# Gate exponents of four mLSTM heads: from selector and mask matmuls to transfers and a GpSimd fill

## The chip, the core and the metric

The kernel runs on one core of one Trainium2 chip. A core has TensorE (PE: matmuls, with the weight load PEld beside it), VectorE (DVE), ScalarE (ACT), GpSimd (POOL) and SyncE (SP), each with its own instruction queue, worked off in order. SP and POOL issue transfers here. The metric is device time in microseconds (us), the median of the runs; lower is better.

## The reference

A trunk of two layers over 512 tokens of width 1024: layer A (four mLSTM heads beside four memory-attention heads, then a gated MLP), layer B (band attention beside memory attention, then a gated MLP), all in float32. The change sits in the mLSTM heads. Per chunk and head the reference computes

```
b = cumsum(lf)                                 # lf: log forget gate, ii: log input gate
d = b[t] - b[s] + ii[s]   where s <= t, else -inf
m_t = max(b + m_st, max_s d)
s = (q k^T) * exp(d - m_t)
num = s v + inter * (q C);   den = sum(s) + inter * (q n)
h = num / max(|den|, exp(-m_t))
```

so each head needs a 512 by 512 lower-triangular matrix of exp(row term + column term): one term depends on the key token s, the other on the query token t, and entries with s > t are zero.

## The kernel before

Every float32 product is made of three float32r matmuls over a high and a low part (`mm3`, lines 176 to 180): high by high (L178), high by low (L179), low by high (L180). The parts come from `split` (lines 133 to 135): ScalarE copies the high part (L134) and VectorE subtracts for the low part (L135). Weights of 512 KB each arrive in three `wr` buffers by SP's queue and are split into three `wh` and three `wl` buffers. PSUM has three `pmm`, three `psc` and two `ptr` banks.

Keys lie on the 128 partitions, in four blocks s = 0 to 3; block s has the queries from s*128 on, so 512, 384, 256 and 128 columns. `gate_rows` (line 1005) makes the gate terms: scans on VectorE on 4 partitions (one per head), then for each block s the row term of each query in `rr`, at 4 partitions of a 128-partition tile (L1053, L1062, VectorE). Lines 1067 to 1071 split these rows into a high and a low part in `rp`, two float32r tiles with zeros elsewhere (memsets L1029 on GpSimd). The column term, on the key partitions, is `acol` (L1075 to L1077, by PE transposes).

In `mlstm_head`, `weighted_scores(s)` puts head h's row term on all 128 partitions with a matmul of a 0/1 selector `sels` against `rp` (L1134, into a `psc` bank), adds a mask of 0 and -1e30 for the block on the diagonal with a second matmul, identity against mask (L1135), and ScalarE takes exp with `acol` as bias out of that bank (L1137). Then PE makes the scores into another `psc` bank (`mm3` and two L517), VectorE multiplies them with the exp (L1143), and the result is split into `pt`. `products(s)` multiplies `pt` with the values into two `ptr` banks. The selectors, the identity and the mask in float32r are made once at the start (lines 101 to 118).

The order on the engines is made by a scheduler from the program's order, except where `pin` keeps it or `manual_schedule` sets it. Each head is a generator whose steps are woven with projections of other tiles (`weave`, lines 1202 to 1223): PE has projection matmuls to do between a head's steps. `gate_rows` is woven with the value projections and the tiles of heads 0 and 1 and finished before head 0 starts. `head_queries` (line 494) needs two GpSimd memsets (L497) for each of its four calls in layer A.

The pool tag `bias` has two buffers of 128 x 512, used only from layer B on (L1301, L1383).

Of the kernel before, what the change touches and what calls it, by code (L numbers as in the profile page):

```python
# [16 lines left out]
P = 128  # L17
D = 1024
S = 512
# [27 lines left out]
def f(ap):  # L47
    return ap.bitcast(F32)
# [3 lines left out]
def trunk(  # L52
# [22 lines left out]
    pool = ctx.enter_context(tc.tile_pool(name="pool", bufs=1))  # L75
    psum = ctx.enter_context(tc.tile_pool(name="psum", bufs=1, space=bass.MemoryType.PSUM))

    bufs = {"wr": 3, "wh": 3, "wl": 3, "u": 57, "t": 8, "pt": 2, "s": 16, "rb": 3, "bias": 2}
    pbufs = {"mm": 3, "sc": 3, "tr": 2}
    count = [0]  # L80
    dram = ctx.enter_context(tc.tile_pool(name="dram", bufs=1, space=bass.MemoryType.DRAM))
# [1 line left out]
    def sb(tag, shape, dtype=F32):  # L83
        count[0] += 1
        return pool.tile(shape, dtype, tag=tag, name=f"{tag}{count[0]}", bufs=bufs[tag])
# [12 lines left out]
    V.memset(ones, 1.0)  # L98
    onesr = cpool.tile([P, P], F32R, name="onesr")
    V.tensor_copy(onesr, ones)  # L100
    identr = cpool.tile([P, P], F32R, name="identr")
    V.tensor_copy(identr, ident)
    maskf = cpool.tile([P, P], F32, name="maskf")
    G.memset(maskf, 0.0)

# [1 line left out]
        out=maskf, in_=maskf, pattern=[[1, P]], base=0, channel_multiplier=-1,  # L107
        compare_op=ALU.is_ge, fill=NEG,
    )
    maskr = cpool.tile([P, P], F32R, name="maskr")  # L110
    V.tensor_copy(maskr, maskf)

    sels = [cpool.tile([P, AH, P], F32R, name=f"sel{i}") for i in range(2)]
    for i, sel in enumerate(sels):
        G.memset(f(sel), 0.0)
        for s in (2 * i, 2 * i + 1):
            q = slice(32 * s, 32 * s + AH)
            V.tensor_copy(sel[q], ident[q, 32 * s : 32 * s + AH].unsqueeze(2).to_broadcast([AH, AH, P]))

    mcf = cpool.tile([P, 3, 2], F32, name="mcf")  # L120
    V.memset(mcf, 0.0)
    V.memset(mcf[:, 0, 0:1], 1.0)
# [78 lines left out]
    def chain(*gens):  # L201
        for g in gens:
            yield from g
# [796 lines left out]
    floor2 = cpool.tile([P, TT, AH], F32, name="floor2")  # L1000
    RO = [0, 512, 896, 1152, 1280]

    rp = []

    def gate_rows():

# [17 lines left out]
        yield  # L1024
        lfr, br, ar, mr = (sb("t", [P, S])[:AH, :] for _ in range(4))
        rr = [sb("t", [P, S]) for _ in range(2)]
        rp.extend(sb("u", [P, S], F32R) for _ in range(2))
        for t in rp:
            G.memset(f(t), 0.0)  # L1029
        pin(V.tensor_copy(lfr, lfp[:AH, :]))  # L1030
        yield
        for T in range(TT):
# [14 lines left out]
        for s in range(TT):  # L1047
            off = None
            for T in range(s, TT):
                sl = slice(T * P, (T + 1) * P)  # L1050
                dst = rr[s // 2][64 * (s % 2) : 64 * (s % 2) + AH, sl]
                if T == s:
                    pin(V.tensor_scalar(dst, mr[:, sl], -1.0, None, op0=ALU.mult))  # L1053
                else:
                    end = br[:, T * P - 1 : T * P]
                    if off is None:
                        off = end
                    else:
                        k = 4 + 4 * s + T - s
                        V.tensor_tensor(out=tot[:, k : k + 1], in0=off, in1=end, op=ALU.add)  # L1060
                        off = tot[:, k : k + 1]
                    V.tensor_scalar(dst, mr[:, sl], -1.0, off, op0=ALU.mult, op1=ALU.add)  # L1062
            yield
        pin(V.tensor_tensor(out=mr, in0=mr, in1=br, op=ALU.add))
        V.tensor_scalar(mr, mr, -40.0, None, op0=ALU.max)
        yield
        for s in range(TT):
            q, t = 64 * (s % 2), rp[s // 2]
            src, hi = rr[s // 2][q : q + AH, s * P :], t[q : q + AH, s * P :]
            pin(V.tensor_copy(hi, src))  # L1070
            V.tensor_tensor(out=t[q + 32 : q + 32 + AH, s * P :], in0=src, in1=f(hi), op=ALU.subtract)
            yield
        tp = ps("tr")
        for T in range(TT):
            nc.tensor.transpose(tp[:, T * AH : (T + 1) * AH], ar[:, T * P : (T + 1) * P], ident[:AH, :AH])  # L1075
# [44 lines left out]
    def a_memory_queries(hp):  # L1120
        memq[hp] = queries((yield from project(w_in, 4 * AW + 2 * AH + hp * P, act)), None)

    def mlstm_head(h):
        hp, odd = divmod(h, 2)
        sh = 3 * hp + 1
# [4 lines left out]
        def weighted_scores(s):  # L1130
            n = S - s * P
            sl = slice(s * P, (s + 1) * P)
            r = ps("sc")
            nc.tensor.matmul(r[:, :n], sels[s % 2][:, h, :], rp[s // 2][:, s * P :], start=True, stop=False)  # L1134
            nc.tensor.matmul(r[:, :P], identr, maskr, start=False, stop=True)  # L1135
            e = sb("t", [P, S])
            A.activation(e[:, :n], r[:, :n], AF.Exp, bias=acol[:, s, h : h + 1])  # L1137
            yield
            o = ps("sc")
            kf, qf = ks[full], qs[full]  # L1140
            mm3(o[:, :n], kf[0][:, sl], kf[1][:, sl], qf[0][:, s * P :], qf[1][:, s * P :], True, False)
            head_scores(o[:, :n], odd, qs[sh], slice(s * P, S), ks[sh], sl, False, True)
            V.scalar_tensor_tensor(e[:, :n], o[:, :n], DH**-0.5, e[:, :n], op0=ALU.mult, op1=ALU.mult)  # L1143
            split(pt[:, RO[s] : RO[s + 1]], pt[:, 1280 + RO[s] : 1280 + RO[s + 1]], e[:, :n])
            yield
# [15 lines left out]
        yield from weighted_scores(2)  # L1161
        yield from products(0)
        yield from weighted_scores(3)
        yield from products(1)
        yield from products(2)
        yield from products(3)
        sqs = []
        for o, j, r in ((nums[0], full, slice(0, P)), (nums[1], sh, rs)):
# [2 lines left out]
            sqs.append(sq)  # L1171
            V.tensor_tensor(out=og[j][r, :], in0=o[r, :], in1=og[j][r, :], op=ALU.mult)
        yield
        st = ps("sc")
        for T in range(TT):
            sl = slice(T * P, (T + 1) * P)
# [25 lines left out]
    fill = gate_rows()  # L1202
    weave(chain(value_columns(0), a_tiles(0, 1)), fill, 0.3)
    run(fill)
    fill = chain(a_tiles(2), a_memory_queries(0), a_tiles(3, 4), a_tiles(5), a_memory_queries(1))
    memkv = load_memory_kv(0)
    weave(mlstm_head(0), fill, 1.4)
# [293 lines left out]
```

## Time and profile before

| what | value |
|---|---|
| median of 3 runs | 1211.98 us (1211.79 to 1214.2) |
| span of the profiled execution, first to last instruction | 1209.9 us |
| TensorE busy | 1196.0 us, 99% of the span, 7063 matmuls |
| VectorE, ScalarE, GpSimd busy | 945.1, 711.1, 125.3 us |
| granted TensorE clock, mean | 0.999 |
| L1134, first and last start | 106.3 (weight load) to 240.2 us, 16 times |

The profile is of one execution. Its own time is given only as the span, 1209.9 us, which lies 2.1 us below the median of the runs; what lies around the span is not itemised. Busy time of TensorE counts a matmul from its start to the end of its pipeline, which overlaps the next one; how fast matmuls follow one another is read from the differences of their starts. A row of the timeline is: start (us), duration (us), engine, line, operation, tiles written and read, shapes, count, and, in brackets, the idle time before it and who ended it.

### The profile page before, as it was taken

How to read it: one execution, taken by the hardware profiler on the slowest of the kernel's cores; microseconds unless marked ns; L12 is line 12 of the kernel's file. 1: busy time of each engine (PE TensorE's matmuls, PEld its weight loads, DVE VectorE, ACT ScalarE, POOL GpSimd, SP SyncE). 2: the span in 40 equal slices, each digit the busy share in tenths (PEclk: the TensorE clock that was granted, in tenths of full speed). 3: DMA queues.
4: the chain of work that ended last, by engine and by line, in shares of the span. 5: the costliest groups of instructions: out<-in, count | busy, mean ns of one | idle time of the engine just before them, and what ended most of it. 6: DMA issues, size and time to landing. Idle time of an engine off the chain costs nothing.

```text
span 1209.9 us, 18791 instructions
## 1 busy us (share of the span) xinstructions
PE 1196.0 (99%) x7063; PEld 1058.6 (87%) x7063; DVE 945.1 (78%) x1733; ACT 711.1 (59%) x1251; POOL 125.3 (10%) x197
## 2 busy tenths in 40 slices
PE   9999999999999999999999999999999999999997
PEld 9988888888889999999988888878889999999986
DVE  7878688877978777777698888997896777777755
ACT  4536577644655555555475667775565555555545
POOL 1300000001011111111011000001101001111100
PEclk9999999999999999999999999999999999999999
DMA  8634111347556676665563323145845466666551
GB/s 276 207 98 122 54 53 57 109 138 187 129 137 160 145 160 150 161 141 133 143 195 109 99 72 94 57 129 167 199 97 139 107 138 139 140 140 134 120 156 70
DMA packets 205260, 159.14 MB, mean 132 GB/s; under 512 B 7960, under 2 KB 185586, under 8 KB 205170
## 3 DMA queue, kind: packets, MB, share of 16 engines
q1 hardware_dynamic: 184338, 120.78, 34.1%
q0 software_dynamic: 20832, 37.17, 16.5%
q8 instruction: 55, 0.90, 0.3%
q14 instruction: 35, 0.29, 0.1%
HBM read 129.42 MB, written 32.44 MB: 134 GB/s over the span
## 4 chain that ended last, share of the span: by engine, by line
PE 94%; ACT 3%; DVE 2%; issue 0%; ACTq 0%; DVEq 0%
PE pmm L178 18%; PE pmm L180 18%; PE pmm L179 18%; PE ptr L178 6%; PE ptr L179 6%; PE ptr L180 6%; PE psc L180 5%; PE psc L178 5%; PE psc L179 5%; PE psc L517 2%; PE ptr L1328 1%; ACT wh L134 1%; PE ptr L1349 1%; PE ptr L1350 1%; PE ptr L586 0%; PE ptr L600 0%
## 5 line engine op out<-in xcount | busy, mean ns | idle before, releaser
L178 PE MATMUL pmm<-u,wh 128*128 128x512 f32 (+1 forms) x968 | 337.1, 349 | 0.1
L180 PE MATMUL pmm<-u,wl 128*128 128x512 f32 (+1 forms) x968 | 333.6, 345 | 0.0
L179 PE MATMUL pmm<-u,wh 128*128 128x512 f32 (+1 forms) x968 | 333.3, 345 | 0.1
L135 DVE TENSOR_TENSOR wl<-wr,wh 128x1024 fp32r<-128x1024 f32 (+4 forms) x168 | 194.7, 1160 | 96.7 <-ACT wh L134 96.0
L134 ACT CAST wh<-wr 128x1024 fp32r<-128x1024 f32 (+4 forms) x168 | 168.0, 1002 | 99.9 <-PE pmm L179 47.2
L180 PEld LDWEIGHTS pmm<-u,wl 128*128 128x128 f32 x968 | 183.6, 190 | 21.1
L179 PEld LDWEIGHTS pmm<-u,wh 128*128 128x128 f32 x968 | 183.9, 190 | 18.0 <-DVE u L135 0.8
L178 PEld LDWEIGHTS pmm<-u,wh 128*128 128x128 f32 x968 | 183.7, 190 | 17.7 <-ACT u L134 0.5
L178 PE MATMUL ptr<-u,wh 128*128 128x512 f32 x272 | 106.7, 392 | 0.0
L179 PE MATMUL ptr<-u,wh 128*128 128x512 f32 x272 | 106.5, 392 | 0.0
L180 PE MATMUL ptr<-u,wl 128*128 128x512 f32 x272 | 105.8, 389 | 0.0
L748 POOL DMA_DIRECT2D xspill<-t x64 | 56.0, 875 | 411.4 <-ACT t L747 408.6
L178 PE MATMUL pmm<-u,u 128*128 128x256 f32 x296 | 84.5, 285 | 2.5 <-ACT t L824 2.5
L180 PE MATMUL pmm<-u,u 128*128 128x256 f32 x296 | 84.0, 284 | 0.4 <-DVE u L135 0.4
L179 PE MATMUL pmm<-u,u 128*128 128x256 f32 x296 | 83.8, 283 | 0.0
L135 DVE TENSOR_TENSOR u<-pt,u 128x512 fp32r<-128x512 f32 x102 | 69.9, 688 | 9.7 <-ACT u L134 7.1
L178 PE MATMUL psc<-u,wh 128*128 128x256 f32 (+1 forms) x232 | 76.1, 328 | 0.0
L179 PE MATMUL psc<-u,wh 128*128 128x256 f32 (+1 forms) x232 | 75.9, 327 | 0.0
L747 ACT COPY t<-ptr 128x512 f32<-128x512 f32 x64 | 37.5, 586 | 65.3 <-PE ptr L180 65.3
L135 DVE TENSOR_TENSOR u<-t,u 128x512 fp32r<-128x512 f32 x78 | 53.4, 689 | 21.4 <-ACT u L134 21.1
L134 ACT CAST u<-pt 128x512 fp32r<-128x512 f32 x102 | 63.2, 619 | 11.4 <-DVE pt L859 11.1
L921 ACT ACTIVATE t<-t 128x512 f32<-128x512 f32 x34 | 21.6, 635 | 80.2 <-DVE t L657 80.2
(290 smaller groups left out, 2568.0 us busy)
## 6 DMA issues: line engine op xcount, KB each, us to landing
wr<-in_ffn_w_up_dram SPq DMA_DIRECT2D x54, 512.0 KB, 5.0
wr<-in_ffn_w_down_dram SPq DMA_DIRECT2D x38, 512.0 KB, 3.8
pt<-in_ffn_w_up_dram SPq DMA_DIRECT2D x34, 512.0 KB, 6.8
xspill<-t POOLq DMA_DIRECT2D x64, 256.0 KB, 4.8
wr<-in_a_w_in_dram SPq DMA_DIRECT2D x20, 512.0 KB, 3.8
xspill<-u POOLq DMA_DIRECT2D x32, 256.0 KB, 3.0
u<-xspill SPq DMA_DIRECT2D x32, 256.0 KB, 4.9
wr<-in_w_kv_dram SPq DMA_DIRECT2D x12, 512.0 KB, 4.1
```

The lines of the kernel that those rows point to most:

```text
L134: high = A.copy(hi, src) if on_act else V.tensor_copy(hi, src)
L135: low = V.tensor_tensor(out=lo, in0=src, in1=f(hi), op=ALU.subtract)
L178: nc.tensor.matmul(o, lh, rh, start=first, stop=False, skip_group_check=more)
L179: nc.tensor.matmul(o, lh, rl, start=False, stop=False, skip_group_check=more)
L180: nc.tensor.matmul(o, ll, rh, start=False, stop=last, skip_group_check=more)
L517: nc.tensor.matmul(o, a, b, start=first and i == 0, stop=i == 1)
L747: A.copy(t, o)
L748: G.dma_start(xspill[j], t, accum_op=ALU.add)
L921: A.activation(self.acc, self.acc, AF.Silu)
L1328: nc.tensor.transpose(tp[:, b * P : (b + 1) * P], es[T, h][:, b * P : (b + 1) * P], ident)
L1349: nc.tensor.matmul(o2[:, s * P :], w, hi_at(pts[h], s, s, TT - s), start=s == 0, stop=False)
L1350: nc.tensor.matmul(o2[:, s * P :], w, lo_at(pts[h], s, s, TT - s), start=False, stop=s == TT - 1)
```

## The change

`gate_rows` no longer splits the rows into `rp`, and the memsets of `rp`, the selectors and the float32r identity and mask are gone. When a block's rows stand in `rr`, GpSimd's queue writes its four rows to a DRAM tile `rowd` (4 transfers). `exponents(h, s)` reads one row back with a step of zero over the partitions, so that all 128 partitions of a `bias` buffer hold it; `masked(h, s)` is a GpSimd affine_select that fills the 128 x 128 block on the diagonal with -1e30 where the query lies before the key. ScalarE's exp reads that buffer instead of a `psc` bank. Head 0's four loads and fills stand before head 0; those of head h+1 stand inside head h, the loads after `weighted_scores(3)`, the fills after its products and squares. The tag `bias` has four buffers.

```
-    bufs = {"wr": 3, "wh": 3, "wl": 3, "u": 57, "t": 8, "pt": 2, "s": 16, "rb": 3, "bias": 2}
+    bufs = {"wr": 3, "wh": 3, "wl": 3, "u": 57, "t": 8, "pt": 2, "s": 16, "rb": 3, "bias": 4}
...
-    identr = cpool.tile([P, P], F32R, name="identr")
-    V.tensor_copy(identr, ident)
...
-    maskr = cpool.tile([P, P], F32R, name="maskr")
-    V.tensor_copy(maskr, maskf)
-
-    sels = [cpool.tile([P, AH, P], F32R, name=f"sel{i}") for i in range(2)]
-    for i, sel in enumerate(sels):
-        G.memset(f(sel), 0.0)
-        for s in (2 * i, 2 * i + 1):
...
-    rp = []
+    rowd = dram.tile([TT, AH, S], F32, name="rowd")
...
-        rp.extend(sb("u", [P, S], F32R) for _ in range(2))
-        for t in rp:
-            G.memset(f(t), 0.0)
...
+            q = 64 * (s % 2)
+            pin(G.dma_start(rowd[s, :, s * P :], rr[s // 2][q : q + AH, s * P :]))
             yield
...
-        for s in range(TT):
-            q, t = 64 * (s % 2), rp[s // 2]
-            src, hi = rr[s // 2][q : q + AH, s * P :], t[q : q + AH, s * P :]
-            pin(V.tensor_copy(hi, src))
-            V.tensor_tensor(out=t[q + 32 : q + 32 + AH, s * P :], in0=src, in1=f(hi), op=ALU.subtract)
-            yield
...
+    exps = {}
+
+    def exponents(h, s):
+
+        n = S - s * P
+        r = sb("bias", [P, S])
+        src = bass.AP(tensor=rowd.tensor, offset=rowd.offset + (s * AH + h) * S + s * P, ap=[[0, P], [1, n]])
+        pin(G.dma_start(r[:, :n], src))
+        exps[h, s] = r
+
+    def masked(h, s):
+
+        r = exps[h, s]
+        pin(
+            G.affine_select(
+                out=r[:, :P], in_=r[:, :P], pattern=[[1, P]], base=0, channel_multiplier=-1,
+                compare_op=ALU.is_ge, fill=NEG,
+            )
+        )
+
...
-            r = ps("sc")
-            nc.tensor.matmul(r[:, :n], sels[s % 2][:, h, :], rp[s // 2][:, s * P :], start=True, stop=False)
-            nc.tensor.matmul(r[:, :P], identr, maskr, start=False, stop=True)
+            r = exps.pop((h, s))
             e = sb("t", [P, S])
             A.activation(e[:, :n], r[:, :n], AF.Exp, bias=acol[:, s, h : h + 1])
...
         yield from weighted_scores(3)
+        for s in range(TT if h < AH - 1 else 0):
+            exponents(h + 1, s)
         yield from products(1)
...
+        for s in range(TT if h < AH - 1 else 0):
+            masked(h + 1, s)
         st = ps("sc")
...
     run(fill)
+    for s in range(TT):
+        exponents(0, s)
+    for s in range(TT):
+        masked(0, s)
```

In the changed file the write is L1049, the load L1111, the fill L1118 and the exp L1136; the other lines named above move by a few numbers.

The first place at which the order moves is GpSimd's queue ahead of head 0. Before (L1029 clears `rp`, L990 and L991 are memsets in value tiles, L497 those of `head_queries`):

```order
L1029 MEMSET u_898 128x512
L1029 MEMSET u_899 128x512
L990 MEMSET u_963 128x128
...
L991 MEMSET u_982 128x128
L497 MEMSET u_1126 64x512
L497 MEMSET u_1127 64x512
L497 MEMSET u_1616 64x512
```

Now, from the last memset of the value tiles on:

```order
L979 MEMSET u_967 128x128
L1049 DMA rowd<-t_885 4x512
L1049 DMA rowd<-t_885 4x384
L1049 DMA rowd<-t_886 4x256
L1049 DMA rowd<-t_886 4x128
L485 MEMSET u_1115 64x512
L485 MEMSET u_1116 64x512
L1111 DMA bias_1247<-rowd 128x512
L1111 DMA bias_1249<-rowd 128x384
L1111 DMA bias_1251<-rowd 128x256
L1111 DMA bias_1253<-rowd 128x128
L1118 AFFINE_SELECT bias_1247<-bias_1247 128x128
```

The writes stand ahead of the first pair of memsets of `head_queries` (L485 here), and the loads and fills of head 0 ahead of everything that follows on this queue.

The second place is ScalarE around head 0's first exp. Before (L1091 is the silu of the last key tile, L1078 a small exp with its table, L507 the copies of that key tile, L1105 the tanh that empties a projection bank):

```order
L134 CAST wh_1374<-wr_1372 128x1024
L1091 ACTIVATE t_1173<-t_1173 128x512
L1078 ACT_TABLE_LOAD
L1078 ACTIVATE floor_596<-ptr_1215 128x16
L507 CAST u_1179<-t_1173 64x512
L507 CAST u_1180<-t_1173 64x512
L1105 ACTIVATE u_1229<-pmm_1191 128x512
L134 CAST wh_1453<-wr_1451 128x1024
L1105 ACTIVATE u_1263<-pmm_1238 128x512
```

Now (the same silu is L1072, the copies L495, the tanh L1086):

```order
L122 CAST wh_1366<-wr_1364 128x1024
L1072 ACTIVATE t_1167<-t_1167 128x512
L1136 ACT_TABLE_LOAD
L1136 ACTIVATE t_1282<-bias_1247,acol 128x512
L495 CAST u_1173<-t_1167 64x512
L495 CAST u_1174<-t_1167 64x512
L1086 ACTIVATE u_1210<-pmm_1185 128x512
L1136 ACTIVATE t_1306<-bias_1249,acol 128x384
L1136 ACTIVATE t_1326<-bias_1251,acol 128x256
L1086 ACTIVATE u_1244<-pmm_1219 128x512
```

Head 0's first exp has moved up, from behind both tanh to directly behind the silu and ahead of the copies of the key tile. The small exp of line 1078 went ahead of the silu of an earlier tile, with a table load of its own behind it.

More of the change, by code (lines that the diff above doesn't have):

```diff
@@ L109, in trunk @@
     )
-    maskr = cpool.tile([P, P], F32R, name="maskr")
-    V.tensor_copy(maskr, maskf)
-    sels = [cpool.tile([P, AH, P], F32R, name=f"sel{i}") for i in range(2)]
-    for i, sel in enumerate(sels):
-        G.memset(f(sel), 0.0)
-        for s in (2 * i, 2 * i + 1):
-            q = slice(32 * s, 32 * s + AH)
-            V.tensor_copy(sel[q], ident[q, 32 * s : 32 * s + AH].unsqueeze(2).to_broadcast([AH, AH, P]))
     mcf = cpool.tile([P, 3, 2], F32, name="mcf")
```

## The prediction

> **What bounds the kernel now.** I read the page first, then the chain of waits on it, then busy times by stretch for the stage of the change, and last the timeline of TensorE there.
>
> ```profile
> span 1209.9 us, 18791 instructions
> PE 1196.0 (99%) x7063; PEld 1058.6 (87%) x7063; DVE 945.1 (78%) x1733; ACT 711.1 (59%) x1251; POOL 125.3 (10%) x197
> ...
> PE 94%; ACT 3%; DVE 2%; issue 0%; ACTq 0%; DVEq 0%
> ```
>
> TensorE is busy for 99% of the span and holds 94% of the chain that ended last. The mLSTM heads run from about 106 to 258 us. The stretches (busy us by engine, in the order PE, PEld, DVE, ACT, POOL, with instruction counts; then clock, DMA share, GB/s):
>
> ```profile
> 80.00:106.00 26.00, 26.00 (x121) 21.35 (x120) 23.25 (x39) 16.68 (x24) 0.00 (x0) 1.00 0.34 97
> 106.00:126.00 20.00, 20.00 (x106) 17.24 (x105) 12.94 (x22) 12.38 (x23) 1.04 (x2) 1.00 0.31 86
> 126.00:150.00 24.00, 24.00 (x128) 20.60 (x127) 18.29 (x42) 13.71 (x22) 1.04 (x2) 1.00 0.24 67
> ...
> 175.00:200.00 25.00, 24.90 (x124) 20.52 (x123) 22.86 (x41) 22.85 (x40) 0.00 (x0) 1.00 0.18 54
> ...
> 225.00:260.00 35.00, 34.86 (x188) 29.29 (x188) 25.59 (x61) 18.77 (x42) 0.00 (x0) 1.00 0.37 118
> ```
>
> TensorE never rests in any of them, GpSimd hardly works, and the DMA engines are two thirds free. Only from 175 to 200 us are ScalarE and VectorE (22.9 of 25 us each) near full. So a matmul taken out of this stage moves the end, unless another engine is just behind.
>
> **What the matmuls cost.** The change takes out 16 pairs, a selector (L1134) and a mask (L1135):
>
> ```profile
> L1134 PE MATMUL psc<-u,sel x16: 222/310/393, 106.5 to 240.2; 128*128 128x512 f32 x4, 128*128 128x384 f32 x4, 128*128 128x256 f32 x4, 128*128 128x128 f32 x4
> ```
>
> The durations (222 to 393 ns) include the pipeline, so I take starts. Head 0's four pairs, with what follows:
>
> ```profile
> 106.31 0.39 PE L180 MATMUL pmm<-u,wl 128*128 128x512 f32 x1
> 106.54 0.39 PE L1134 MATMUL psc<-u,sel 128*128 128x512 f32 x1
> 106.77 0.22 PE L1135 MATMUL psc<-maskr,identr 128*128 128x128 f32 x1
> 106.83 0.44 PE L178 MATMUL pmm<-u,wh 128*128 128x512 f32 x1
> 107.11 0.40 PE L179 MATMUL pmm<-u,wh 128*128 128x512 f32 x1
> ...
> 109.43 0.34 PE L1134 MATMUL psc<-u,sel 128*128 128x384 f32 x1
> ...
> 109.66 0.44 PE L178 MATMUL pmm<-u,wh 128*128 128x512 f32 x1
> 109.94 0.39 PE L179 MATMUL pmm<-u,wh 128*128 128x512 f32 x1
> ...
> 112.69 0.28 PE L1134 MATMUL psc<-u,sel 128*128 128x256 f32 x1
> ...
> 112.86 0.44 PE L178 MATMUL pmm<-u,wh 128*128 128x512 f32 x1
> 113.15 0.40 PE L179 MATMUL pmm<-u,wh 128*128 128x512 f32 x1
> ...
> 117.63 0.22 PE L1134 MATMUL psc<-u,sel 128*128 128x128 f32 x1
> ...
> 117.80 0.45 PE L178 MATMUL pmm<-u,wh 128*128 128x512 f32 x1
> 118.09 0.39 PE L179 MATMUL pmm<-u,wh 128*128 128x512 f32 x1
> ```
>
> A plain 512-column matmul holds the place for 0.23 us (106.31 to 106.54). From selector to next matmul the pairs hold it for 0.29, 0.23, 0.17 and 0.17 us, 0.86 together. The matmul behind each pair then takes 0.28, 0.28, 0.29 and 0.29 to its successor in place of 0.23: 0.05 + 0.05 + 0.06 + 0.06 = 0.22 more, since its successor's weights load late behind the short mask matmul. That makes 0.86 + 0.22 = 1.08 us a head, **4.3 us** for four heads. Lower bound 3.4 (4 x 0.86), if the matmul behind stays slow because of another short one.
>
> The Trainium skill, "TensorE: Matmul & The Clock Gate", section "Back-to-back issue gap", gives N / 2.4 + 2.5 ns for isolated matmuls in a warm stream. By it the 16 pairs would be about 3.1 us, an estimate from that page. The trace has more (0.29 us for 512 + 128 columns against 0.27 by the rule, and the slow successor), and the rows decide.
>
> **What of it is given back.** One place in the stage shows TensorE waiting, though it counts as busy there:
>
> ```profile
> 190.68 0.39 PE L180 MATMUL pmm<-u,wl 128*128 128x512 f32 x1
> 191.17 0.73 PE L517 MATMUL psc<-u,u 128*128 128x512 f32 x2
> ...
> 166.75 1.06 ACT L134 CAST wh<-wr 128x1024 fp32r<-128x1024 f32 x1 [1.72 <-PE pmm L179]
> ...
> 189.77 1.26 ACT L507 CAST u<-t 64x512 fp32r<-64x512 f32 x2
> ...
> 190.42 0.69 DVE L508 TENSOR_TENSOR u<-t,u 64x512 fp32r<-64x512 f32 x1 [0.59 <-ACT u L507]
> ```
>
> The gap from 190.68 to 191.17 is 0.49 in place of 0.23: head 2's first scores wait 0.26 us for the low part of its key tile (L508), behind ScalarE's L507. ScalarE works almost without a break from 166.75 to that point, and it began because TensorE let go of a buffer. What heads 0 and 1 save lies ahead of 166.75 and moves this whole chain forward. Head 2's first pair stands between (its scores begin at this wait), so its 0.29 + 0.05 = **0.34 us** becomes more waiting. The sum is 4.3 - 0.3 = **4.0 us saved**.
>
> **What is added, and what hides it.** Head 0 is the tight case. Rows and stand-ins for the new work:
>
> ```profile
> 83.52 0.22 DVE L1053 TENSOR_SCALAR t<-t 4x128 f32<-4x128 f32 x1
> ...
> 101.05 1.06 ACT L134 CAST wh<-wr 128x1024 fp32r<-128x1024 f32 x1 [1.37 <-PE pmm L179]
> 102.19 0.64 ACT L1091 ACTIVATE t<-t 128x512 f32<-128x512 f32 x1
> 102.85 1.28 ACT L1078 ACT_TABLE_LOAD   x1
> ...
> L1201 POOL DMA_DIRECT2D xspill<-u x8: 542/542/543, 41.3 to 45.0; - x8
> ...
> DMA to landing us min/median/max: 2.3/5.4/6.0
> ...
> L106 POOL TENSOR_SCALAR_AFFINE_SELECT maskf<-maskf x1: 284/284/284, 1.4 to 1.4; 128x128 f32<-128x128 f32 x1
> ```
>
> The last gate row is done at 83.74 (83.52 + 0.22). No row times a 4-partition write or a zero-step load; the nearest are GpSimd's eight spills of 256 KB, 0.54 us to issue and 2.3 to 6.0 to land. The last write is issued by 84.3 and lands between 86.6 and 90.3. The last load then takes 0.54 and the same range again: 89.4 to 96.8. The four fills (0.28 each, 1.1) end between 90.5 and **97.9**. ScalarE reaches the first exp in the new order behind the same silu and a table load: 102.19 + 0.64 + 1.28, about **104**. So the fills are at least 6 us early, the cost is nothing, and the cover is those 6 us. Behind the exp on ScalarE wait L507's copies, for which head 0's scores on TensorE wait; a late exp would stall them one for one. The exp here takes the place of the small exp of L1078, so L507 moves by about half a microsecond (0.69 for 0.18), and its scores stood about 2 us behind it.
>
> For heads 1 to 3 the loads are issued when the head before has let go of the buffers:
>
> ```profile
> 118.00 0.37 ACT L1137 ACTIVATE t<-psc,acol 128x128 f32<-128x128 f32 x1 [0.71 <-PE psc L1135]
> ...
> 134.56 1.28 ACT L1137 ACT_TABLE_LOAD   x1
> ```
>
> From the end of head 0's last exp (118.37) to head 1's table load are 16.2 us, the shortest such pause of the three; the worst case is 0.54 x 4 + 6.0 + 1.1 = 9.3. Hidden. The memsets of `head_queries` now queue behind these fills on GpSimd, and their readers on VectorE come later still.
>
> The additions off the path: GpSimd gets 20 issues at 0.54 (10.9 us) and 16 fills at 0.28 (4.5), 15.4 us beside 125 in all; it loses four memsets. ScalarE gets two more table loads of 1.28 around 92 to 104 us, where it has 9.3 of 26 us idle. VectorE loses the eight small splits, and the casts at the start, which end before anything there waits for them. The exp's source is SBUF in place of PSUM, taken at the same price. Each at nothing: TensorE is covered by weight casts that run as far ahead as the buffers let them (the one at 101.05 waited 1.37 us for TensorE); without that cover the two table loads would cost it up to 2.6 us. The two more `bias` buffers let the loads of layer B start earlier, where no engine is shown waiting for them.
>
> **Rivals.**
>
> (1) *The other engines keep the pace.* If ScalarE's chain up to 190 us did not start earlier, all that heads 0 and 1 and head 2's first pair save (2 x 1.08 + 0.34 = 2.5) would end in the wait at 190.68, and 4.3 - 2.5 = 1.8 would be left: 1210.2. For it: 22.85 of 25 us busy. Against it: the row at 166.75, released by TensorE.
>
> (2) *GpSimd holds VectorE up*, and the kernel is slower. The fills read and write SBUF beside VectorE's subtractions. The trace knows one lengthened form:
>
> ```profile
> L577 DVE TENSOR_SCALAR t<-t,s x32: 335/348/695, 173.7 to 803.2; 128x256 f32<-128x256 f32 x32
> ...
> 763.52 1.80 POOL L497 MEMSET u<- 64x512 f32 x3 [23.50 <-PE pmm L180]
> 763.90 0.96 DVE L577 TENSOR_SCALAR t<-t,s 128x256 f32<-128x256 f32 x2
> ```
>
> Two of these, 0.348 each as a rule, take 0.96 while GpSimd's memsets run. If every fill and issue held VectorE for its length, 15.4 us, and two thirds of that reached TensorE, 10.3 - 4.0 = 6.3 would be lost: 1218.3. It decides from 6.4 us on (4.0 plus 2.4). Against it: VectorE has 2 to 7 us idle in each stretch, and its work is mostly ahead of TensorE. The Trainium skill, "SBUF — State Buffer", section "Who interferes with whom", says that a VectorE operation with two SBUF inputs contends with a GpSimd instruction that reads SBUF; a fill does, and the subtractions are such operations. By it each fill could hold one subtraction, and no run here shows it yet, since in this profile such fills ran only at the very start.
>
> (3) *Head 0's rows come late.* If the two hops took 6 + 2 us longer than the worst case above, each further microsecond stalls head 0's scores; at 4 us beyond, the gain is gone: 1212.
>
> (4) *More than the matmuls goes.* A `psc` bank less per block could also end the 0.26 us wait and small ones at the heads' ends: 5.0 us, 1207.0.
>
> **How the numbers follow.** The sum is made against the profiled execution, span 1209.9, so 1205.9 expected there. The median of the runs shown is 1211.98, 2.1 above, and I take the same off it: **1208.0**. A measurement here can tell about 0.2%, 2.4 us. Chances: forecast 0.62 (its own range 3.0 to 5.0 saved), rival (1) 0.18, (2) 0.06, (3) 0.06, (4) 0.08. Faster by more than 2.4: the forecast, (4), and a third of (3), 0.72; within: (1) and a third of (3), rounded up, 0.21; slower: the rest, 0.07. The range 1206.0 to 1212.0 runs from a little beyond (4) to (3).
>
> **What would show it.** Right: no L1134 or L1135 groups; TensorE's starts run at 0.23 us through the heads; the first exp (L1136) starts near 104 with its fill done by 98 and no wait on GpSimd; the stage ends about 4 us earlier, and nothing changes after. A wait of TensorE of 0.6 us at head 2's first scores would confirm the piece given back; one of 2.7 would mean rival (1). Longer subtractions (L135) beside fills mean (2); ScalarE idle, released by GpSimd, ahead of L1136 means (3). The prediction is wrong if TensorE's waits in this stage grow by over 1.6 us, or if later stages, which the change leaves alone, move by as much.

## The result: 4 us faster, and what the profile after shows

| kernel | median, us (runs) | kernel before beside it | ratio, 95% interval |
|---|---|---|---|
| changed | 1208.28 (5) | 1212.42 (5) | 0.9964 [0.9952, 0.9976] |
| changed, a second set | 1208.05 (11) | 1211.67 (17) | 0.9975 [0.9966, 0.9984] |

The predicted 1208.0 is met to 0.3 us. The traces say that it was met with two errors of opposite sign: the stage of the heads gained more than the sum had, and the start lost time that the sum did not have. That they nearly cancel is luck. The head of the page of the changed kernel, and the group of its new loads, fills and exponentials (their tile is `bias`):

```profile
span 1206.5 us, 18758 instructions
PE 1191.2 (99%) x7031; PEld 1055.1 (87%) x7031; DVE 938.8 (78%) x1719; ACT 711.9 (59%) x1253; POOL 139.5 (12%) x229
...
PE 94%; ACT 3%; DVE 2%; DMA 0%; issue 0%; SPq 0%; DVEq 0%; ACTq 0%
```

```profile
L1111 POOL DMA_DIRECT2D bias<-rowd x16: 535/554/754, 87.8 to 199.4; - x16
L1118 POOL TENSOR_SCALAR_AFFINE_SELECT bias<-bias x16: 282/292/567, 92.4 to 202.8; 128x128 f32<-128x128 f32 x16
L1136 ACT ACTIVATE t<-bias,acol x16: 389/562/725, 105.9 to 237.9; 128x512 f32<-128x512 f32 x4, 128x384 f32<-128x384 f32 x4, 128x256 f32<-128x256 f32 x4, 128x128 f32<-128x128 f32 x4
...
DMA to landing us min/median/max: 3.2/3.9/8.0
```

TensorE has 32 matmuls less and still fills 99% of the span. GpSimd is busy 14.2 us longer: 16.3 us of added issues and fills, for which 15.4 was the estimate, less the four memsets that are gone.

**The stage.** TensorE's projection and score matmuls are as many in both kernels (6282 of lines L178 to L180, now L166 to L168), so the same one can be found in both. One shortly before head 0 and one behind head 3, first in the kernel before, then in the changed one (start us, duration us, engine, line, operation, tiles, shapes):

```profile
103.82 0.39 PE L178 MATMUL pmm<-u,wh 128*128 128x512 f32 x1
...
279.85 0.39 PE L179 MATMUL pmm<-u,wh 128*128 128x512 f32 x1
```

```profile
105.71 0.39 PE L166 MATMUL pmm<-u,wh 128*128 128x512 f32 x1
...
277.08 0.39 PE L167 MATMUL pmm<-u,wh 128*128 128x512 f32 x1
```

The changed kernel reaches the first one 1.89 us *later* and the second one 2.77 us *earlier*. From the one to the other are 176.03 us before and 171.37 now: the stage gained 4.66 us, not 4.0. Behind it another 0.6 us is gained, which need not be the change's: the kernel before with nothing but a transfer moved at its start (below) gains the same there (0.66), and over all the profiles of this document that part takes between 929.3 and 931.0 us, in no order that follows the changes. 1.89 - 4.66 - 0.6 = -3.4, the difference of the spans.

**The start.** Of the 1.89 us, 1.69 are lost in the first 12 us, matmul against matmul; the other 0.2 come near 55 us and are not followed here. The kernel before at its start, and the changed one (rows of the timeline; the brackets give the idle time and who ended it):

```profile
1.62 0.98 POOL L115 MEMSET sel<- 128x512 f32 x2
...
2.56 0.73 POOL L332 DMA_DIRECT2D gateb<-in_a_gate_b_dram  x1
...
5.50 0.66 PE L441 MATMUL psc<-ident,u 128*128 128x128 f32 x4
```

```profile
1.66 0.72 POOL L320 DMA_DIRECT2D gateb<-in_a_gate_b_dram  x1
...
7.76 0.66 PE L429 MATMUL psc<-ident,u 128*128 128x128 f32 x4 [1.77 <-DMA u<-in_mem_dram]
```

The second group of transposes, which feeds the first products of the program, waits 1.77 us for a load of the memory rows. What changed ahead of it is on GpSimd: the two selector memsets (L115, 0.98 us) are gone, and GpSimd issues the transfer of the gate bias `gateb`, 32 bytes to each of 128 partitions (L332, now L320), at 1.66 us in place of 2.56. Of the four loads of the memory rows, which SyncE issues at 0.75, 1.75, 2.77 and 3.79 us, it now precedes three instead of two. The traffic of the DMA engines in the first 10 us, in 40 slices of 0.25 us, and the share of the queue that carries `gateb` (q0), before:

```profile
GB/s 0 0 0 0 0 0 0 53 233 365 295 213 270 360 279 238 270 320 275 287 270 247 250 261 240 232 237 179 145 172 225 270 311 373 381 381 385 381 385 385
...
q0 software_dynamic: 32, 0.00, 1.9%
```

and changed:

```profile
GB/s 0 0 0 0 0 0 0 94 168 319 328 307 344 365 283 107 185 110 127 42 3 38 117 202 221 242 315 377 377 377 385 389 361 377 361 348 365 336 352 365
...
q0 software_dynamic: 32, 0.00, 7.8%
```

Around 5 us the traffic falls to 3 GB/s; before, no slice from 2 to 10 us is under 145. That the early transfer does this is, so far, an inference from one pair of traces.

### The profile page after: what moved, and what is told of

Same layout as the page of the kernel before. It is cut to its first block, busy times and chain, and to the rows that moved or that the text cites. A ratio compares the mean times of both kernels' runs of the same rounds, so it can differ in the third digit from the quotient of the medians.

```text
span 1206.5 us, 18758 instructions
## 1 busy us (share of the span) xinstructions
PE 1191.2 (99%) x7031; PEld 1055.1 (87%) x7031; DVE 938.8 (78%) x1719; ACT 711.9 (59%) x1253; POOL 139.5 (12%) x229
## 4 chain that ended last, share of the span: by engine, by line
PE 94%; ACT 3%; DVE 2%; DMA 0%; issue 0%; SPq 0%; DVEq 0%; ACTq 0%
PE pmm L166 18%; PE pmm L168 18%; PE pmm L167 18%; PE ptr L166 6%; PE ptr L167 6%; PE ptr L168 6%; PE psc L168 5%; PE psc L167 5%; PE psc L166 5%; PE psc L505 2%; PE ptr L1335 1%; ACT wh L122 1%; PE ptr L1356 1%; PE ptr L1357 1%; DMA u<-in_mem_dram 0%; PE ptr L574 0%
## 5 line engine op out<-in xcount | busy, mean ns | idle before, releaser
L166 PE MATMUL pmm<-u,wh 128*128 128x512 f32 (+1 forms) x968 | 336.6, 348 | 0.1
L168 PE MATMUL pmm<-u,wl 128*128 128x512 f32 (+1 forms) x968 | 333.5, 345 | 0.0
L168 PEld LDWEIGHTS pmm<-u,wl 128*128 128x128 f32 x968 | 183.6, 190 | 21.1
L166 PEld LDWEIGHTS pmm<-u,wh 128*128 128x128 f32 x968 | 183.7, 190 | 18.0 <-ACT u L122 0.5
L166 PE MATMUL ptr<-u,wh 128*128 128x512 f32 x272 | 106.7, 392 | 0.0
L168 PE MATMUL ptr<-u,wl 128*128 128x512 f32 x272 | 105.8, 389 | 0.0
L166 PE MATMUL pmm<-u,u 128*128 128x256 f32 x296 | 84.5, 285 | 2.5 <-ACT t L812 2.5
L168 PE MATMUL pmm<-u,u 128*128 128x256 f32 x296 | 83.9, 284 | 0.2 <-DVE u L123 0.2
L166 PE MATMUL psc<-u,wh 128*128 128x256 f32 (+1 forms) x232 | 76.1, 328 | 0.0
```

What stands on the lines that cost most here:

```text
L166: nc.tensor.matmul(o, lh, rh, start=first, stop=False, skip_group_check=more)
L168: nc.tensor.matmul(o, ll, rh, start=False, stop=last, skip_group_check=more)
```

## Experiments at the start: whose time was lost

**Theory S**: the selector memsets had kept the gate bias transfer out of the way of the first loads, and their removal costs what the start lost. **Rival R**: something else in the start changed, or the load was late by chance.

### The changed kernel with the gate bias transfer later

```
-    G.dma_start(gateb, bass.AP(tensor=a_gate_b.tensor, ...))
...
+    pin(G.dma_start(gateb, bass.AP(tensor=a_gate_b.tensor, ...)))
     run(value_columns(1))
```

> The changed kernel with one thing moved: GpSimd issues the 4 KB transfer of the gate bias to all partitions (gateb) behind the four spills of the memory keys, about 40 us later, instead of as its first transfer at 1.66 us; its reader stands near 60 us. Theory S (the two selector memsets that the change removes used to hold this transfer back by 0.9 us; without them it runs into the first loads of the memory rows, whose traffic falls to 3 to 42 GB/s around 5 us, and TensorE waits 1.77 us at 7.76 us): the wait before the second group of transposes is gone, the transposes start near 5.5 us as in the kernel before or earlier, and the median is 1.6 to 1.9 us under the changed kernel's 1208.3: 1206.4 to 1206.7. Rival R (the late row landing has another cause, such as VectorE's missing casts, or one slow transfer by chance): the wait stays and the median stays within 0.5 us of 1208.3.

Measured: 1206.73 us (5 runs), ratio to the kernel before 0.996 [0.9947, 0.9972]. The median is 0.03 us above the range of S, but the profiled execution was the slowest of the five (1209.38) and waited too:

```profile
7.34 1.11 PE L428 MATMUL psc<-ident,u 128*128 128x128 f32 x4 [1.21 <-DMA u<-in_mem_dram]
...
8.68 0.41 PE L168 MATMUL pmm<-u,u 128*128 128x256 f32 x1
8.89 0.41 PE L166 MATMUL pmm<-u,u 128*128 128x256 f32 x1
```

So the loads can be late without the transfer as well. And the 256-column matmuls here follow one another at 0.21 us, against 0.12 in the changed kernel at the same place; they run so until 10.2 us. With both, the matmul before head 0 starts at 106.48 us, 2.5 us later than in the next profile of the same kernel (104.00). One set could not settle it.

### The same once more, beside the changed kernel itself

> The changed kernel with the gate bias transfer 40 us later, once more, since its profiled execution (1209.38, wait of 1.2 us in the start) was the slowest of its five and the other four had 1206.5 to 1207.3. Theory S: a median 1.3 to 1.9 us under the changed kernel's beside it, and a start without a wait of over 0.5 us in most executions. Rival R2 (the loads at the start land late in some executions whatever the gate bias transfer does, and the first medians differed by chance): the same median as the changed kernel's within 0.5 us.

> The changed kernel unaltered, beside the others on one chip. Theory S: 1207.9 to 1209.0 as before, with TensorE's wait of 1 to 2 us before the second group of transposes in the profile.

Measured: 1207.09 us (5 runs, 1206.32 to 1207.22) for the later transfer, 1208.05 us (11 runs, 1207.45 to 1211.16) for the changed kernel unaltered. The two starts:

```profile
5.74 0.60 PE L428 MATMUL psc<-ident,u 128*128 128x128 f32 x4
```

```profile
6.91 0.66 PE L429 MATMUL psc<-ident,u 128*128 128x128 f32 x4 [0.95 <-DMA u<-in_mem_dram]
```

The difference of the medians is 0.96 in this set, under the 1.3 that S had asked for, and 1.55 between the first sets. Rival R2's 0.5 is exceeded in both.

### The changed kernel with the memsets' time put back

```
-    G.memset(maskf, 0.0)
+    for _ in range(8):
+        tc.keep_in_program_order(G.memset(maskf, 0.0))
...
-    G.dma_start(gateb, bass.AP(tensor=a_gate_b.tensor, ...))
+    pin(G.dma_start(gateb, bass.AP(tensor=a_gate_b.tensor, ...)))
```

The transfer is also pinned to its place behind them.

> The changed kernel with seven more memsets of 128x128 on GpSimd (the same zeros into the same mask tile) ahead of the gate bias transfer, so that it is issued about 0.9 us later, near 2.6 us, as in the kernel before. Theory S: the start is as in the kernel before again, TensorE's second transposes start near 5.5 us, and the median is 1.6 to 1.9 us under 1208.3. Rival R: no change from 1208.3, the wait of 1.8 us stays.

Measured: 1206.97 us (5 runs), ratio 0.9958 [0.9945, 0.997], 1.3 us under the changed kernel's 1208.28, where S had asked for 1.6 to 1.9. The memsets took longer than planned (2.10 us), so the transfer went out at 3.82 us, not 2.6:

```profile
1.27 2.10 POOL L103 MEMSET maskf<- 128x128 f32 x8
...
3.82 0.72 POOL L321 DMA_DIRECT2D gateb<-in_a_gate_b_dram  x1
...
5.50 0.66 PE L430 MATMUL psc<-ident,u 128*128 128x128 f32 x4 [0.35 <-DMA u<-in_mem_dram]
```

Useless work on an idle engine makes the kernel faster here, since it delays what that engine issues next.

### The transfer issued twice

```
     G.dma_start(gateb, bass.AP(tensor=a_gate_b.tensor, ...))
+    gateb2 = cpool.tile([P, 2 * AH], F32, name="gateb2")
+    G.dma_start(gateb2, bass.AP(tensor=a_gate_b.tensor, ...))
```

> The changed kernel with the 4 KB gate bias transfer issued twice in a row at the start, the second into a tile that nothing reads. Theory S (this transfer's small packets hold the first loads back): the dip in the DMA engines' traffic around 5 us gets longer, the second row load lands later, and the median is 0.7 to 2 us above the changed kernel's 1208.1: 1208.8 to 1210. Rival R2 (the start's waits come from elsewhere): 1208.1 within 0.5 us.

Measured: 1208.98 us (11 runs, 1207.47 to 1211.86), within the range of S, 0.9 us above the changed kernel of the second set. The two sets of runs overlap widely, so the medians alone do not show the 0.9. The trace shows the dose more clearly. The queue's share is 13.7%, against 3.8 to 10.3% in the six traces with a single transfer at 1.66 us, the median landing of the memory rows 7.7 us against 5.1 to 6.0, and TensorE waits 3.58 us:

```profile
GB/s 0 0 0 0 0 0 0 45 156 344 356 238 295 360 320 214 170 116 54 113 55 37 66 158 213 180 176 200 154 194 252 279 291 266 283 378 373 373 385 385
...
q0 software_dynamic: 64, 0.01, 13.7%
...
9.52 0.69 PE L431 MATMUL psc<-ident,u 128*128 128x128 f32 x2 [3.58 <-DMA u<-in_mem_dram]
```

Not all of this execution's delay is the wait: from 9.0 to 12.4 us its granted clock was 0.50, so TensorE also ran slowly behind it.

### The kernel before with the transfer later

> The kernel before with the same move of the gate bias transfer. It parts the start from the stage of the heads. Theory S: the kernel before loses little to this transfer (its packets took 1.9% of the DMA engines' time in the first 10 us against 7.8% in the changed kernel), and TensorE's only wait there is 0.21 us: 0 to 1 us under the kernel before, 1211.4 to 1212.4. The distance to the changed kernel with the same move is then the worth of the heads' stage by itself: 4.7 to 5.2 us. Rival R: the same time as the kernel before, and a distance of 4.1.

Measured: 1211.36 us (11 runs) against 1211.8, ratio 0.9995 [0.9987, 1.0004]: at most a small gain, and none is shown, which fits S and R alike. The stage takes as long as in the kernel before (176.0 us). The two kernels with the later transfer differ by 1211.36 - 1206.73 = 4.6 us in this set or, with the second set's later transfer, 4.3; S expected 4.7 to 5.2 and R 4.1. By itself this run does not decide between them.

**What follows.** With the early transfer four sets of runs (the two of the changed kernel and two below that leave the length of the heads' stage as it is) have medians of 1208.05 to 1208.48; with the transfer late or held back four sets (two here, the memsets, and one below) have 1206.73 to 1207.09. In the one set that has both, all five runs with the later transfer (1206.32 to 1207.22) are faster than all eleven of the changed kernel (from 1207.45).

The traces agree. With one transfer at 1.66 us, the traffic between 3 and 8 us falls to between 3 and 92 GB/s in each of six profiles, and the second group of transposes starts at 6.91 to 7.76 us; with the transfer at 2.56 us or later, no slice there is under 144 GB/s in any of seven, and the transposes start at 5.34 to 5.86 us in five.

S holds, with a price of about 1.3 us between the medians. It is not the only cause of late loads: the two exceptions among the seven are the first profile above (7.34) and the kernel with doubled pairs, below, which waited 1.32 us (6.70) with the transfer at 2.56.

## Experiments in the heads' stage: where the 4.66 us come from

### The additions taken away

The row writes, the row loads and the fills are left out; the exponentials read a tile of ones, so the row terms and the causal mask are missing from what is computed.

```
-            pin(G.dma_start(rowd[s, :, s * P :], rr[s // 2][q : q + AH, s * P :]))
...
-            r = exps.pop((h, s))
-            A.activation(e[:, :n], r[:, :n], AF.Exp, bias=acol[:, s, h : h + 1])
+            flat = ones.unsqueeze(1).to_broadcast([P, n // P, P])
+            A.activation(e[:, :n].rearrange("p (a b) -> p a b", b=P), flat, AF.Exp, bias=acol[:, s, h : h + 1])
...
-        for s in range(TT if h < AH - 1 else 0):
-            exponents(h + 1, s)
...
-    for s in range(TT):
-        masked(0, s)
```

> The changed kernel without any of the added work: no row writes, no row loads, no fills; the exponentials read a tile of ones in their place, so the row terms and the causal mask are left out of the result. The start is the changed kernel's. The prediction's theory (all additions are hidden behind other work): the same time as the changed kernel within 0.3 us, 1208.0 to 1208.6. Rival 2 (GpSimd holds VectorE up) or a cost of the extra DMA traffic: faster than the changed kernel by 1 us or more, below 1207.3.

Measured: 1208.48 us (6 runs), ratio 0.9969 [0.9957, 0.9981]; within the 0.3 us of the prediction's theory. TensorE's order of instructions is the changed kernel's. Its two matmuls:

```profile
106.21 0.39 PE L166 MATMUL pmm<-u,wh 128*128 128x512 f32 x1
...
277.60 0.39 PE L167 MATMUL pmm<-u,wh 128*128 128x512 f32 x1
```

171.39 us from the one to the other, as with the transfers and fills (171.37). Four writes, 16 loads and 16 fills cost TensorE nothing.

### The pairs doubled

```
             nc.tensor.matmul(r[:, :n], sels[s % 2][:, h, :], rp[s // 2][:, s * P :], start=True, stop=False)
             nc.tensor.matmul(r[:, :P], identr, maskr, start=False, stop=True)
+            nc.tensor.matmul(r[:, :n], sels[s % 2][:, h, :], rp[s // 2][:, s * P :], start=True, stop=False)
+            nc.tensor.matmul(r[:, :P], identr, maskr, start=False, stop=True)
```

> The kernel before with each of the 16 selector and mask pairs issued twice in a row into the same tile (the second starts the sum anew, so the result is the same). It prices the pairs by themselves. Prediction's sum: 4 x 0.86 in place = 3.4 us at the least, up to 4.3 with the slow successors; a pair behind a pair pays the late weights once more behind the short mask matmul: 3.4 to 4.8 us above the kernel before. Rival (more than the matmuls goes with the change, a bank's wait for example): under 3.0 us, since doubling the matmuls adds none of those waits.

Measured: 1217.18 us (5 runs) against 1211.67, 5.5 above, ratio 1.0044 [1.0032, 1.0057]: more than any of the theories asked for. In the stage alone, by the same two matmuls:

```profile
104.44 0.39 PE L178 MATMUL pmm<-u,wh 128*128 128x512 f32 x1
...
107.16 0.39 PE L1134 MATMUL psc<-u,sel 128*128 128x512 f32 x1
107.39 0.22 PE L1135 MATMUL psc<-maskr,identr 128*128 128x128 f32 x1
107.45 0.44 PE L1136 MATMUL psc<-u,sel 128*128 128x512 f32 x1
107.73 0.22 PE L1137 MATMUL psc<-maskr,identr 128*128 128x128 f32 x1
107.79 0.44 PE L178 MATMUL pmm<-u,wh 128*128 128x512 f32 x1
...
284.98 0.39 PE L179 MATMUL pmm<-u,wh 128*128 128x512 f32 x1
```

180.54 us, 4.5 more than in the kernel before (176.03). The first pair takes 0.29 us, the second 0.34 (107.45 to 107.79), since its selector now stands behind a short mask matmul and is itself the slow successor. The stage's 4.5 us for sixteen pairs are within the theory's 3.4 to 4.8. The other 1 us of the median lies outside the heads: in the profiled execution 0.6 at the start and 0.9 behind the stage, and why the five runs share it stays open.

### The fills four times each

```
         r = exps[h, s]
-        pin(G.affine_select(out=r[:, :P], in_=r[:, :P], ..., compare_op=ALU.is_ge, fill=NEG))
+        for _ in range(4):
+            pin(G.affine_select(out=r[:, :P], in_=r[:, :P], ..., compare_op=ALU.is_ge, fill=NEG))
```

> The changed kernel with each of the 16 causal fills done four times in a row on GpSimd (the later three change nothing). 48 more fills of 0.29 us, 13.9 us. Prediction's theory: hidden, the changed kernel's time within 0.4 us, VectorE's subtractions beside fills stay at 0.69 us. Rival 2 (a fill holds VectorE up for its length and two thirds of that reach TensorE): 9 us slower; with half of that, 4 us.

Measured: 1208.35 us (7 runs), ratio 0.9974 [0.9963, 0.9984]. The stage takes 171.39 us (105.05 to 276.44), unchanged. Rival 2 of the prediction, GpSimd holding VectorE up, asked for 4 to 9 us and falls. The contention that it rests on is there, though, and goes mostly the other way. The group of fills, one fill, and the subtraction beside it:

```profile
L1119 POOL TENSOR_SCALAR_AFFINE_SELECT bias<-bias x64: 284/295/1314, 92.3 to 204.5; 128x128 f32<-128x128 f32 x64
```

```profile
92.19 1.22 DVE L123 TENSOR_TENSOR wl<-wr,wh 128x1024 fp32r<-128x1024 f32 x1
...
92.29 1.27 POOL L1119 TENSOR_SCALAR_AFFINE_SELECT bias<-bias 128x128 f32<-128x128 f32 x1 [3.00 <-DMA bias<-rowd]
```

A fill is 0.29 us as a rule. This one, begun 0.10 us behind a subtraction of two SBUF tiles, lasts 1.27, to 0.15 us past the subtraction's end; the subtraction keeps its 1.22. The Trainium skill, "SBUF — State Buffer", section "Who interferes with whom", says that such an operation contends with a GpSimd instruction that reads SBUF, and that the order of issue decides which of the two blocks. The trace agrees for the fill, 1.27 in place of 0.29. Fifteen of the 64 fills took over 0.32 us. VectorE pays less: of its subtractions that overlap a fill some take about 0.1 us longer (one of 512 columns 0.77 us in place of 0.68, two of 256 columns 0.51 in place of 0.42, one of 1024 columns 1.33 in place of 1.22). The prediction named longer subtractions as the sign of rival 2; they are there, but none of it reaches TensorE. Mostly it is GpSimd that pays, and GpSimd has time.

### Head 0's rows later

Memsets on GpSimd, into the first row tile, hold head 0's loads back (30 of them, then 44):

```
+        for _ in range(30 if h + s == 0 else 0):
+            pin(G.memset(r, 0.0))
         pin(G.dma_start(r[:, :n], src))
```

> The changed kernel with 30 memsets of 128x512 (0.49 us each, 14.7 us; each writes zeros into the first row tile ahead of its load) on GpSimd between the row writes and head 0's row loads. In the changed kernel the first fill is done at 92.73 us and the first exponential starts at 105.86: cover 13.1 us for the first block (8.1 for the last fill). With 14.7 us more the first row is 1.6 us late. Prediction's theory (behind a late exponential head 0's scores have about 2 us more of cover, then TensorE stalls one for one): 0 to 0.6 us above the changed kernel, 1207.9 to 1208.7, with ScalarE idle 1 to 2 us ahead of the first exponential, released by GpSimd. Rival (the rows are needed well before the exponential, or the memsets hold VectorE up): 2 us or more above it.

> The same with 44 memsets, 21.6 us: the first row is 8.5 us late. Prediction's theory: TensorE stalls 8.5 - 2 = 6.5 us before head 0's scores and gets nothing of it back: 1214 to 1215.5, slower than the kernel before (1211.7). Rival (other ready work keeps TensorE busy, since fill work is woven between the head's matmuls): 3 us or less, under 1211.5.

Measured: 1210.03 us (10 runs) and 1214.61 us (8 runs). The first number misses the range of the prediction's theory (to 1208.7) and comes to the edge of the rival's (2 us or more). The second is inside the expected range, and for a reason other than the expected one. The memsets followed one another at 0.59 us, not 0.49, so the delays were 17.6 and 26.2 us:

```profile
86.79 26.20 POOL L1112 MEMSET bias<- 128x512 f32 x44
```

And the order of TensorE's and ScalarE's instructions, which is worked out anew for every kernel, had moved head 0's exponentials and scores back to suit. Against the changed kernel's first profile, an execution at its median, the profiled execution with 30 memsets (1209.66) lost 0.4 us ahead of the stage, 0.5 in it and 0.5 behind it, 1.4 in all; why the median of the ten runs lies 1.8 to 2.0 us higher stays open. With 44 the stage lost 7.1 us (178.55 against 171.4), hardly any of it at head 0. TensorE waited 0.84 us ahead of head 1's scores. From 158 to 162 us its granted clock was 0.58 in the mean, half for 3.4 of these 4 us. Between 189 and 192.5 it waited on the exponentials of the memory attention (L562) and what follows from them:

```profile
158.00:162.00 4.00, 4.00 (x12) 3.15 (x11) 3.56 (x18) 1.91 (x2) 0.00 (x0) 0.58 0.00 0
```

```profile
144.09 0.50 PE L242 MATMUL psc<-t,onesr 128*128 128x512 f32 x1 [0.84 <-DVE t L229]
...
190.35 0.39 PE L166 MATMUL psc<-u,u 128*128 128x256 f32 x1 [0.84 <-ACT t L562]
...
192.46 0.72 PE L588 MATMUL ptr<-pt,u 128*128 128x512 f32 x2 [0.80 <-DVE pt L123]
```

What the delay of head 0's rows has to do with these three places is not shown. So these two runs do not test the stall "one for one": the order never let it come about. Both theories are left undecided by them. A smaller delay, on top of the later gate bias transfer, keeps TensorE's order as it is in the changed kernel:

> The changed kernel with the gate bias transfer 40 us later (1206.7 and 1207.1 in two sets), and 16 memsets of 128x512 (0.59 us each as measured, 9.4 us) on GpSimd between the row writes and head 0's row loads. Unlike 30 or 44 of them, 16 leave TensorE's order of instructions as it is in the changed kernel; ScalarE's order moves the first exponentials behind a few weight casts. Theory C (each exponential needs only its own fill, 12 to 13 us of cover in the changed kernel): no time lost in the heads' stage, 1206.4 to 1207.4. Rival (the cover is the 6 us of the prediction, or the 8.1 us from the last fill to the first exponential, and TensorE stalls for what goes beyond it and its own 2 us): 1 to 2 us more, 1208 to 1209.

Measured: 1207.03 us (5 runs), ratio 0.9961 [0.9947, 0.9974], as without the memsets. The first and the last of head 0's fills and its exponentials:

```profile
99.49 0.29 POOL L1119 TENSOR_SCALAR_AFFINE_SELECT bias<-bias 128x128 f32<-128x128 f32 x1 [1.76 <-DMA bias<-rowd]
...
104.42 0.72 POOL L1119 TENSOR_SCALAR_AFFINE_SELECT bias<-bias 128x128 f32<-128x128 f32 x1 [0.72 <-DMA bias<-rowd]
...
111.22 1.63 ACT L1137 ACTIVATE t<-bias,acol 128x512 f32<-128x512 f32 x3
```

The first fill came 8.4 us later than with the same start and no memsets (99.49 against 91.12), and no time was lost; the stage takes 171.43 us. The rival's 1 to 2 us did not come. Theory C is not shown by it in full, though: ScalarE's order was made anew here too and put the first exponential at 111.22 instead of 104.19, 6 us behind the end of the last fill, with TensorE none the worse. How a late row would stall a *fixed* order was not tried, since the order does not stay as it is when something ahead of it grows.

## Why the prediction was right, and where it was wrong

**The bound was right.** Matmuls taken out of the heads moved the end of the heads, and the doubling and the removal agree: 4.5 us for sixteen pairs put in, 4.66 for sixteen taken out.

**The pairs were mis-sized, 4.3 for 4.64.** The step took head 0's 1.08 us four times. The same reading of starts over all 16 pairs of the kernel before, against a plain spacing of 0.227 us in place of the rounded 0.23, gives 1.10, 1.14, 1.10 and 1.30 for heads 0 to 3, together 4.64: 3.65 in place and 0.99 by slow successors. Head 3's pairs stood between short matmuls and cost more. The stage gained between 4.60 and 4.67 in each of eight traces: the changed kernel twice, four with only the start altered, the one without the additions and the one with four times the fills. The estimate of 3.1 us by the Trainium skill, "TensorE: Matmul & The Clock Gate", section "Back-to-back issue gap", falls short by a third: of the 1.5 us that are missing, 0.99 are the slow successors, and the rest is in the pairs themselves. The rows were the right choice.

**The piece given back, 0.34, did not come.** The step let TensorE arrive 0.34 us earlier at head 2's first scores and wait the longer for them. In the changed kernel (before: 190.68 and 191.17):

```profile
187.13 0.33 PE L166 MATMUL psc<-u,u 128*128 128x384 f32 x1
...
190.28 0.39 PE L166 MATMUL pmm<-u,wh 128*128 128x512 f32 x1
190.71 0.74 PE L505 MATMUL psc<-u,u 128*128 128x512 f32 x2
...
189.32 1.26 ACT L495 CAST u<-t 64x512 fp32r<-64x512 f32 x2
```

The gap is 0.43 us, a wait of 0.20, not 0.6. ScalarE's cast came 0.45 us earlier by the clock (189.77 before); counted from the matmul before head 0, which is 1.89 us late here, it came 2.34 us earlier. So ScalarE's chain moved forward by what heads 0 and 1 saved (2.24 by the starts), as the step had it and against rival (1). But between head 2's place of the first pair and these scores TensorE now has two matmuls more, a 384-column one of the next block's scores (0.17) and one projection (0.23): 0.40 us of other work where the pair's 0.34 had been. The order had been made anew, and the step treated it as fixed but for the missing rows. That the fourth rival ("more than the matmuls goes") named a freed `psc` bank as a cause is not shown by this: why the order chose these two is not in the trace.

**The additions at nothing were right.** The kernel without them has the same stage. The first exponential was put near 104 us; it starts at 105.86, which less the 1.89 us of the start is 103.97. The fills were to be done by 97.9 and the last ends at 97.78, or 95.89 less the same:

```profile
92.44 0.29 POOL L1118 TENSOR_SCALAR_AFFINE_SELECT bias<-bias 128x128 f32<-128x128 f32 x1 [2.50 <-DMA bias<-rowd]
...
97.49 0.29 POOL L1118 TENSOR_SCALAR_AFFINE_SELECT bias<-bias 128x128 f32<-128x128 f32 x1 [1.39 <-DMA bias<-rowd]
...
104.57 1.28 ACT L1136 ACT_TABLE_LOAD   x1
105.86 0.72 ACT L1136 ACTIVATE t<-bias,acol 128x512 f32<-128x512 f32 x1
```

The cover was undercounted all the same: each exponential needs only its own fill, and the first one's is done at 92.73, 13 us ahead. The smallest distance from a fill's end to its exponential is 12.8 us in head 0 and 20 us in the others. The landing was underrated: 3.2 to 8.0 us for the loads, where 6.0 was the worst assumed. And the prediction's sentence that no row times a zero-step load is wrong. Two rows of its profile do: the load of 128x512 in L1385 (0.55 us to issue, 5.2 to land) and the gate bias itself in L332 (0.73 and 5.1).

**The start at nothing was wrong.** The step that failed is the sentence that GpSimd "loses four memsets" and VectorE its casts at the start, which "end before anything there waits for them". Nothing waited for their results. But behind the two selector memsets, in GpSimd's queue, stood a transfer, and what it met when it went out earlier was not looked at. In the changed kernel's two traces this start came 1.7 and 0.8 us later than before; between medians the early transfer costs about 1.3. The prediction named a sign by which it would be wrong, later stages moving by over 1.6 us; it did not name an earlier one.

**The sum as it should have been**: 4.64 for the pairs, nothing given back, nothing for the additions, less about 1.3 for the start, of which the kernel before already paid perhaps 0.4 (not clear of noise): 3.7 us. The two sets of runs gave 4.1 and 3.6. Rivals (1) and (2) are excluded by the stage; (3) did not occur; (4) had the stage's size nearly right (5.0) and would have been the better forecast of the stage alone, but by luck: the matmuls by themselves are 4.64 of the 4.66, and its freed bank is not needed.

**A version faster than both** is the changed kernel with the gate bias transfer issued behind the spills: 1206.73 and 1207.09 us, 4.6 to 5.1 us under the kernel before.

## What to carry to other kernels

When work is removed from an idle engine, read its queue: what stands behind the removed instruction now goes out earlier, and if that is a transfer, ask what it meets on the way. When a scheduler makes the order, a removed instruction's time is not simply given back at the next wait; compare the orders around that wait before costing it. Price a repeated removal on all its places, not on one times their number: the pairs of the last head cost a fifth more than those of the first.

## What was not expected of the hardware

A transfer of 4 KB in all, 32 bytes to a partition, at 1.66 us among loads of 256 KB took 7.8% of the DMA engines' time in the first 10 us (3.8 to 10.3% in six traces), against 1.9% at 2.56 us, and with it the traffic fell to 3 GB/s for a quarter of a microsecond. What goes on inside the engines is not shown.

At the start TensorE can run at half its rate: 0.21 us between starts of 256-column matmuls until 10.2 us in the first profile with the later transfer, 0.12 us from 8.4 us on in the changed kernel. The windows view gives 1.00 for the granted clock all through this slow stretch, but the trace's record of it begins only at 10.34 us there (5.69 in the changed kernel), and time without a record counts as full. The Trainium skill, "TensorE: Matmul & The Clock Gate", section "Part 1: The HAM clock gate", describes a clock of one half that is lifted after a free-running window of sustained work, so that the same kernel starts with a varying number of slow matmuls. The trace agrees (256 columns at half of 2.4 GHz would be 0.213 us, an estimate from that page), and it is a part of the 2.5 us between the two profiles of the kernel with the later transfer. TensorE is still at half rate past 10 us in three of the seven profiles with the early transfer (one of them with the transfer doubled) and in one of the seven others. Whether an early transfer lengthens the slow stretch, and the stretch is thereby a part of the 1.3 us, is open.
